# A two-layer decoder trunk on one core: gate products behind the value projection, kept weight blocks from the MLP's twelfth block on, and four of the inverse's eight late stores on GpSimd's queue

## The chip, the cores and the metric

The kernel runs on one core of a Trainium2 chip. The metric is the device time of one execution in microseconds, the median of several runs.

## The reference, cut to what matters

A trunk of two layers on 512 tokens of 1024 features, in float32. Layer 0 is sparse attention, layer 1 an RWKV-7 mixer; each is followed by an MLP with a squared ReLU of 4096 hidden features. The change touches the first MLP and the RWKV mixer:

```python
def sqrelu_mlp(h, w_up, w_down):
    u = jax.nn.relu(h @ w_up)
    return (u * u) @ w_down
...
r, k, v = jnp.einsum('cbld,cde->cble', xs[:3], w_rkv)
...
g = jax.nn.sigmoid(xg @ g1) @ g2
...
def step(state, inp):                      # over the 512 tokens, 16 heads of 64
    r_t, w_t, k_t, v_t, kk_t, b_t = inp
    sa = jnp.einsum('bhvk,bhk->bhv', state, -kk_t)
    state = (state * w_t[:, :, None, :] + sa[..., None] * b_t[:, :, None, :]
             + v_t[..., None] * k_t[:, :, None, :])
    y = jnp.einsum('bhvk,bhk->bhv', state, r_t)
    return state, y
...
out = (y + bonus).reshape(B, L, D).astype(h.dtype) * g
return out @ w_o
```

## The kernel before, in words

**Weights.** All weights come as blocks of 128 x 1024 float32 in one stream, in the order of the table `c.order`. `wdma` (L92) loads one or two blocks on SyncE's (SP's) queue; `wload` splits a block into a high part by a copy on ScalarE (L109) and a low part by a subtraction on VectorE (L117); `gemm` (L135 to L137) makes 24 matmuls of a block. `wget` keeps two blocks ahead, always in stream order, so the splits stand in that order on ScalarE and VectorE too. 24 blocks of the RWKV mixer (the list `PRE`) are split early: the table puts them in pairs into the first MLP's part of the stream, `pos` marks them, and `keep` (L79) stores both halves of each into DRAM (tiles `scr`) by GpSimd's (POOL's) queue. Later SP loads them back (L85), 1 MB each.

**The first MLP** (`mlp`). For each half of the hidden features, 16 blocks of the first product, m = 0 to 15, each followed by the activations of `act`: VectorE L287, ScalarE L289 and L290, VectorE L291. Then eight products down, of two blocks each. `keep` is called behind every fourth block m of the first product and behind every second of the second one, in the first half only. In the stream, position 26 is the MLP's first block.

**The RWKV mixer.** Tokens go in eight chunks of 64. For each chunk and head, a triangular 64 x 64 matrix has to be inverted, by blocks of 32. `back` (L1015) masks the matrices into the tiles `Mt`; `invert` puts them into DRAM (`dn`, L1029, eight stores for the first eight heads, eight for the others) and loads them back with one matrix per partition (`tn`, L1034, one load for each half f of the chunks). 60 VectorE operations (L1041, L1043) invert all of them. Copies (L1049) and stores and loads through DRAM (`dm`, `dt`) bring the results back as `Mt` and `T11`. Meanwhile PE makes the value projection (192 matmuls, L1229 to L1231, eight PSUM banks) with inputs prepared on VectorE and ScalarE (L753, L120, L117, L751), and `opl` and `opt` make the operands of a chunk: products on PE (L1201, L1202), masks on VectorE (L1196), transposes (L1213) with copies (L1214, and `cp`: L1133 on VectorE, L1135 on ScalarE). Each of these steps has its place in the queues from priorities and the scheduler, up to the line `c.tc.manual_schedule`.

**From there on all five engines follow the order in which the code is written.** First come the copies of the values (`vcopy`, L1241), the gate products (`g2`, L1259 to L1262, 4 matmuls for each of 8 parts), and the preparation of the first chunk: `step_z` (L1290, copied into `bd` by ScalarE L1292), `merge1` (L1143), `merge2` (L1155, copied into `Mt` by ScalarE L1135). Then the loop over the chunks n: `step_z`, `step_u` (L1298, copied by ScalarE L1302), `merge1` of the next, `step_s` and `step_n` (L1309, L1316: the next state), `step_r` (L1327) and `step_y` (L1340, copied by ScalarE L1345: the output), `opl` of the next, `merge2`, `opt`.

PSUM has two pools: four banks "g" and two double banks "d". A tile waits until the one that had its bank has been read.

Of the kernel before, what the change touches and what calls it, by code (L numbers as in the profile page):

```python
# [7 lines left out]
F32 = mybir.dt.float32  # L8
F32R = mybir.dt.float32r
AF = mybir.ActivationFunctionType  # L10
# [266 lines left out]
def mlp(c, x, mi, done, mid, keep=0):  # L277
    nc = c.nc
    c.ph = 'm'
    a = mi.a  # L280
    rstd = None
    wait = []

    @c.site("mact")
    def act(p, hi, lo):
        r = c.t("r")
        nc.vector.scalar_tensor_tensor(r, p, 0.0, rstd, op0=OP.max, op1=OP.mult)  # L287
        q = c.t("q")
        nc.scalar.activation(hi, r, AF.Square)  # L289
        nc.scalar.activation(q, r, AF.Square)  # L290
        nc.vector.tensor_sub(lo, q, hi.bitcast(F32))  # L291

    for half in range(2):
        s = Act(c, "s", 16)
        for m in range(16):
            p = c.bank("g")
            c.gemm(p, c.wget(), a)
            if m % 4 == 3:
                c.keep(keep)
            wait.append((p, *s(m)))  # L300
            if rstd is None:
                if m == 0:
                    mi.n.stat()
                    continue
                rstd = mi.n.spread()
            while wait:
                act(*wait.pop(0))
        for m in range(KC - HM if half else KC):
            p = c.bank("g")
            c.gemm(p, c.wget(), s, last=False)  # L310
            c.gemm(p, c.wget(), lambda k: s(k + 8), first=False)
            if m % 2 and not half:
                c.keep(keep)
            xm = x[m // 4][:, m % 4, :]
            nc.vector.tensor_add(xm, p, xm)  # L315
            if half:
                for h in range(2):
                    done(m, xm[:, HB[h]], h)
    w = [c.wget(1) for _ in range(2 * HM)]
    for h in range(2):  # L320
        for i in range(HM):
            m = KC - HM + i
            p = c.bank("g")[:, :256]
            for j in range(2):
                c.gemm(p, w[2 * i + j], lambda k: [v[:, HB[h]] for v in s(k + 8 * j)], j == 0, j == 1)
                if h:
                    next(mid, None)
            xm = x[m // 4][:, m % 4, HB[h]]
            nc.vector.tensor_add(xm, p, xm)
            done(m, xm, h)  # L330
    for _ in mid:
        pass
# [453 lines left out]
def rwkv(c, x, ks, gi):  # L786
# [232 lines left out]
    def invert():  # L1019
        dn, dm = (c.dram.tile([2, 2, 2, 32, 32, 32], F32, name=v) for v in ("dn", "dm"))  # L1020
        dt = c.dram.tile([2, 2, 32, 32, 32], F32, name="dt")
        mt = [t.rearrange("p q n t -> p (q n) t") for t in Mt]
        for q in range(2):
            qs = slice(16 * q, 16 * q + 16)
            for f in range(2):
                for e in range(2):
                    for b in range(2):
                        r = slice(e * 64 + b * 32, e * 64 + b * 32 + 32)
                        nc.sync.dma_start(dn[f, e, b, qs].rearrange("h i j -> i h j"),  # L1029
                                          mt[f][r, qs, b * 32:b * 32 + 32])  # L1030
            yield HOLD
        tn = c.b8("tn", F32, (128, 2, 32, 32))
        for f in range(2):
            nc.sync.dma_start(tn[:, f].rearrange("p i j -> p (i j)"), dn[f].rearrange("e b h i j -> (e b h) (i j)"))  # L1034
        yield HOLD
        pr = c.t("pr")
        for k in range(30, 0, -1):
            nr = 31 - k
            sh = [128, 2, k, nr]
            pv = pr[:, :2 * k * nr].rearrange("p (f a b) -> p f a b", f=2, a=k)  # L1040
            nc.vector.tensor_mul(pv, tn[:, :, 0:k, k:k + 1].to_broadcast(sh),  # L1041
                                 tn[:, :, k:k + 1, k + 1:].to_broadcast(sh))
            nc.vector.tensor_add(tn[:, :, 0:k, k + 1:], tn[:, :, 0:k, k + 1:], pv)  # L1043
            yield 4 * (k * nr * 1.04 + 65)
        for f in range(2):
            nc.vector.memset(tn[:, f].rearrange("p i j -> p (i j)")[:, 0:1024:33], 1.0)
            tt = [c.t("tt").rearrange("p (i j) -> p i j", j=32) for _ in range(2)]
            for g in range(2):
                nc.vector.tensor_copy(tt[g], tn[:, f].rearrange("p i j -> p j i")[:, 16 * g:16 * g + 16])  # L1049
            if f == 0:  # L1050
                stage.append(0)
                yield HOLD
            nc.sync.dma_start(dm[f].rearrange("e b h i j -> (e b h) (i j)"), tn[:, f].rearrange("p i j -> p (i j)"))
            for e in range(2):
                for g in range(2):
                    nc.sync.dma_start(dt[f, e, :, 16 * g:16 * g + 16], tt[g][e * 64:e * 64 + 32])
            yield HOLD
            T11[f] = [c.t("T11").rearrange("p (h j) -> p h j", j=32) for _ in range(2)]
            for e in range(2):
                for g in range(2):  # L1060
                    nc.sync.dma_start(T11[f][g][e * 64:e * 64 + 32],
                                      dt[f, e, g * 16:(g + 1) * 16].rearrange("h i j -> i h j"))
                for b in range(2):
                    r = slice(e * 64 + b * 32, e * 64 + b * 32 + 32)
                    nc.sync.dma_start(mt[f][r, :, b * 32:b * 32 + 32], dm[f, e, b].rearrange("h i j -> i h j"))
            yield HOLD
# [360 lines left out]
    def opn(n, j):  # L1427
        if j == 0:
            BL[n] = c.b8("BL", F32, (128, 2, 8, 128))
        opl(n, j)  # L1430

    with c.tc.manual_schedule(engines=set(MAN)):
        while not stage:
            run(1)
        until(0)
        for i in VL[:3]:
            vcopy(i)
        vmean(0)
        vload(0)
        opn(1, 0)  # L1440
        for i in VL[3:]:
            vcopy(i)
        del ps
        opn(1, 1)
        (ah, al_), (bh, bl) = ((a.rearrange("p a b -> p (a b)") for a in c.wget(0)) for _ in range(2))
        nc.scalar.activation(bh[64:96], bl[64:96].bitcast(F32), AF.Copy)
        g2(0)
        g2(1)
        step_z(0)
        g2(2)  # L1450
        g2(3)
        opt(1, (0, 0))
        vload(1)
        g2(4)
        g2(5)
        sa[0] = merge1(0)
        g2(6)
        merge2(0, sa[0])
        g2(7)
        for n in range(NCH - 1):  # L1460
            more = True
            if n:
                step_z(n)
            if n % 2 and more:
                vmean((n + 1) // 2)
            if n == 1:
                lnw = g3(c.t("lnw"))
                nc.sync.dma_start(lnw, c.aps["lnw"])
            if n and more:
                acopy(n + 1)  # L1470
                opn(n + 1, 0)
                vload(n + 1)
            if n == 6:
                turn(3)
            for k in GB.get(n, ()):
                gB(k)
            step_u(n)
            if n == 0:
                until(1)
            if more and n != 3:  # L1480
                sa[n + 1] = merge1(n + 1)
            for k in GB.get(n, ()):
                gC(k)
            if more:
                pn = step_s(n)
                step_n(n, pn)
            py = step_r(n)
            if more:
                sbd(n)
            step_y(n, py)  # L1490
            for k in GB.get(n, ()):
                gD(k)
            if n == 6:
                w0 = out(0)
                pull(w0, 1)
            if n and more:
                opn(n + 1, 1)
            if n == 6:
                pull(w0, 2)
            if n == 3:  # L1500
                sa[4] = merge1(4)
            if more:
                merge2(n + 1, sa[n + 1])
            if n and n < NCH - 2:
                opt(n + 1, (0, 0) if n < 3 else TE)
            for k in TU.get(n, ()):
                turn(k)
            for k in GA.get(n, ()):
                gA(k)
            if n == PF1:  # L1510
                c.prefetch(2)
# [130 lines left out]
def build(tc, aps, out):  # L1642
    with ExitStack() as ctx:
# [4 lines left out]
        for i in range(26, BASE):  # L1648
            od.append(i)
            pos.append(0)  # L1650
            if i % 4 == 1:
                pos += [1] * len(pre[:2])
                od += pre[:2]
                del pre[:2]
# [43 lines left out]
```

## Time and profile before

| | |
|---|---|
| median of 3 runs | 1360.39 us (1356.75 to 1364.64) |
| profiled execution | 1363.17 us, its span 1361.0 us |
| mean granted TensorE clock | 0.982 |
| PE busy | 1294.1 us, 95% |
| DVE, ACT, POOL busy | 778.1, 593.5, 191.8 us |
| first MLP | about 265 to 620 us |
| inverse and value projection | about 774 to 827 us |
| chunk loop | about 845 to 960 us |

The table is read with the span: the rows further down come from the one profiled execution and are times from the start of its span. "Busy" counts matmuls for PE; the weight loads run beside them. The granted clock is a share of 2.4 GHz.

### The profile page before, as it was taken

How to read it: one execution, taken by the hardware profiler on the slowest of the kernel's cores; microseconds unless marked ns; L12 is line 12 of the kernel's file. 1: busy time of each engine (PE TensorE's matmuls, PEld its weight loads, DVE VectorE, ACT ScalarE, POOL GpSimd, SP SyncE). 2: the span in 40 equal slices, each digit the busy share in tenths (PEclk: the TensorE clock that was granted, in tenths of full speed). 3: DMA queues.
4: the chain of work that ended last, by engine and by line, in shares of the span. 5: the costliest groups of instructions: out<-in, count | busy, mean ns of one | idle time of the engine just before them, and what ended most of it. 6: DMA issues, size and time to landing. Idle time of an engine off the chain costs nothing.

```text
span 1361.0 us, 20178 instructions
## 1 busy us (share of the span) xinstructions
PE 1294.1 (95%) x8197; PEld 1060.0 (78%) x8197; DVE 778.1 (57%) x1345; ACT 593.5 (44%) x1016; POOL 191.8 (14%) x220
## 2 busy tenths in 40 slices
PE   7989899999999999999999998877999999999997
PEld 6756666878888888899667776766988888888887
DVE  5689983646542556428889785564754532245423
ACT  5545693434432345316875315755343421234421
POOL 0375750001101010000000001253200000000000
PEclk9989999989999999999999998988999999999998
DMA  7101004345677666413241375127131223322401
GB/s 290 63 23 40 1 14 173 116 155 216 228 270 245 246 220 254 144 63 124 78 155 40 94 286 108 28 80 279 53 103 62 93 95 108 108 92 93 155 1 62
DMA packets 73404, 172.09 MB, mean 126 GB/s; under 512 B 33760, under 2 KB 36448, under 8 KB 69472
## 3 DMA queue, kind: packets, MB, share of 16 engines
q1 hardware_dynamic: 64160, 143.41, 30.8%
q0 software_dynamic: 6912, 25.17, 5.1%
q10 hardware_dynamic: 2240, 2.24, 0.5%
q8 instruction: 64, 1.05, 0.3%
q14 instruction: 28, 0.23, 0.0%
HBM read 136.72 MB, written 31.98 MB: 124 GB/s over the span
## 4 chain that ended last, share of the span: by engine, by line
PE 79%; DVE 12%; ACT 4%; issue 2%; DMA 2%; POOL 1%; SPq 1%; DVEq 0%; ACTq 0%; POOLq 0%
PE g L137 20%; PE g L135 20%; PE g L136 20%; PE g L648 2%; DVE rot L431 1%; DVE tn L1043 1%; DVE pr L1041 1%; PE d L633 1%; DVE acc L517 1%; DVE L L607 1%; DVE m L515 1%; PE g L1298 1%; PE g L1013 1%; ACT bd L1292 1%; PE d L406 1%
## 5 line engine op out<-in xcount | busy, mean ns | idle before, releaser
L117 DVE TENSOR_TENSOR w<-wraw,w 128x1024 fp32r<-128x1024 f32 x185 | 224.2, 1239 | 125.9 <-ACT w L109 125.9
L109 ACT ACTIVATE w<-wraw 128x1024 fp32r<-128x1024 f32 x190 | 193.0, 1048 | 141.4 <-DMA wraw<-in_wblk 119.1
L135 PE MATMUL g<-sh,w 128*128 128x512 f32 (+1 forms) x608 | 216.5, 356 | 0.0
L136 PE MATMUL g<-sl,w 128*128 128x512 f32 (+1 forms) x608 | 216.1, 355 | 0.0
L137 PE MATMUL g<-sh,w 128*128 128x512 f32 (+1 forms) x608 | 216.1, 355 | 0.0
L135 PE MATMUL g<-ah,w 128*128 128x512 f32 x512 | 201.0, 393 | 2.9 <-ACT w L109 2.9
L137 PE MATMUL g<-ah,w 128*128 128x512 f32 x512 | 200.3, 391 | 0.0
L136 PE MATMUL g<-al,w 128*128 128x512 f32 x512 | 200.3, 391 | 0.0
L289 ACT ACTIVATE sh<-r 128x512 fp32r<-128x512 f32 x64 | 40.4, 631 | 205.3 <-DVE r L287 205.3
L136 PEld LDWEIGHTS g<-sl,w 128*128 128x128 f32 x608 | 114.9, 189 | 16.4
L135 PEld LDWEIGHTS g<-sh,w 128*128 128x128 f32 x608 | 114.9, 189 | 16.2
L137 PEld LDWEIGHTS g<-sh,w 128*128 128x128 f32 x608 | 114.9, 189 | 16.2
L135 PEld LDWEIGHTS g<-ah,w 128*128 128x128 f32 x512 | 96.8, 189 | 23.1 <-ACT w L109 3.3
L137 PEld LDWEIGHTS g<-ah,w 128*128 128x128 f32 x512 | 96.8, 189 | 21.0 <-DVE w L117 0.8
L136 PEld LDWEIGHTS g<-al,w 128*128 128x128 f32 x512 | 96.9, 189 | 20.1
L287 DVE SCALAR_TENSOR_TENSOR r<-g,rstd 128x512 f32<-128x512 f32 x64 | 44.1, 691 | 82.1 <-PE g L137 70.5
L291 DVE TENSOR_TENSOR sl<-q,sh 128x512 fp32r<-128x512 f32 x64 | 44.4, 694 | 75.4 <-ACT q L290 75.4
L195 ACT ACTIVATE sq<-x 128x256 f32<-128x256 f32 (+1 forms) x56 | 26.7, 499 | 98.1 <-DVE x L315 52.2
L79 POOL DMA_DIRECT2D scr<-w x48 | 25.6, 536 | 295.9 <-ACT w L109 285.8
L315 DVE TENSOR_TENSOR x<-g,x 128x512 f32<-128x512 f32 x26 | 17.9, 690 | 80.6 <-PE g L137 80.6
L617 ACT ACTIVATE L<-L,st 128x256 f32<-128x256 f32 (+3 forms) x64 | 35.1, 552 | 15.1 <-DVE st L615 15.1
L290 ACT ACTIVATE q<-r 128x512 f32<-128x512 f32 x64 | 39.4, 615 | 0.0
(317 smaller groups left out, 2425.7 us busy)
## 6 DMA issues: line engine op xcount, KB each, us to landing
wraw<-in_wblk SPq DMA_DIRECT2D x94, 1024.0 KB, 5.0
scr<-w POOLq DMA_DIRECT2D x48, 512.0 KB, 4.1
w<-scr SPq DMA_DIRECT2D x24, 1024.0 KB, 6.7
wraw<-in_wblk SPq DMA_DIRECT2D x5, 512.0 KB, 3.9
x<-in_xT SPq DMA_DIRECT2D x8, 256.0 KB, 5.3
x<-in_xT SPq DMA_DIRECT2D x2, 1024.0 KB, 6.6
xs<-x SPq DMA_DIRECT2D x2, 1024.0 KB, 5.0
abd<-AR SPq DMA_DIRECT2D x64, 32.0 KB, 2.6
```

What stands on the lines that cost most here:

```text
L109: s.wsp = s.nc.scalar.activation(hi, r, AF.Copy)
L117: s.nc.vector.tensor_sub(out, a, b)
L135: s.nc.tensor.matmul(p, whi[:, kc, :], ahi, start=first and kc == 0, stop=False)
L136: s.nc.tensor.matmul(p, whi[:, kc, :], alo, start=False, stop=False)
L137: s.nc.tensor.matmul(p, wlo[:, kc, :], ahi, start=False, stop=last and kc == KC - 1)
L195: nc.scalar.activation(sq, xk, AF.Square)
L287: nc.vector.scalar_tensor_tensor(r, p, 0.0, rstd, op0=OP.max, op1=OP.mult)
L289: nc.scalar.activation(hi, r, AF.Square)
L290: nc.scalar.activation(q, r, AF.Square)
L291: nc.vector.tensor_sub(lo, q, hi.bitcast(F32))
L617: nc.scalar.activation(L[g][:, :n], L[g][:, :n], AF.Exp, bias=nmx[:, g:g + 1], scale=0.125, accum_out=sm[:, g:g + 1])
L648: nc.tensor.matmul(po[HF[e]], v[sc // 2][:, j:j + 64], st8[tb, pr, e][:, sc], start=sc == 0, stop=sc == tb)
```

## The change

The diff has four parts. In `mlp`, `keep` is called in the second half too; in the table, the pairs of kept blocks start at position 37 instead of 29, and end at 81 instead of 73. In `invert`, the four stores of the last eight whose e is 1 go to GpSimd's queue. Behind the value projection, the weights of the gate products are fetched first, all eight `vcopy` and four `g2` come before the operands of chunk 1, and the rest follows in another order. In the chunk loop, `step_r` is called before `step_u`.

```diff
@@ mlp
-            if m % 2 and not half:
+            if m % 2:
                 c.keep(keep)
@@ invert
-                        nc.sync.dma_start(dn[f, e, b, qs].rearrange("h i j -> i h j"),
+                        (nc.gpsimd if q and e else nc.sync).dma_start(dn[f, e, b, qs].rearrange("h i j -> i h j"),
                                           mt[f][r, qs, b * 32:b * 32 + 32])
@@ rwkv
     with c.tc.manual_schedule(engines=set(MAN)):
+        (ah, al_), (bh, bl) = ((a.rearrange("p a b -> p (a b)") for a in c.wget(0)) for _ in range(2))
+        nc.scalar.activation(bh[64:96], bl[64:96].bitcast(F32), AF.Copy)
         while not stage:
             run(1)
         until(0)
-        for i in VL[:3]:
+        for i in VL:
             vcopy(i)
+        del ps
         vmean(0)
         vload(0)
+        for m in range(4):
+            g2(m)
         opn(1, 0)
-        for i in VL[3:]:
-            vcopy(i)
-        del ps
-        opn(1, 1)
-        (ah, al_), (bh, bl) = ((a.rearrange("p a b -> p (a b)") for a in c.wget(0)) for _ in range(2))
-        nc.scalar.activation(bh[64:96], bl[64:96].bitcast(F32), AF.Copy)
-        g2(0)
-        g2(1)
-        step_z(0)
-        g2(2)
-        g2(3)
-        opt(1, (0, 0))
-        vload(1)
         g2(4)
         g2(5)
+        step_z(0)
+        opn(1, 1)
+        vload(1)
         sa[0] = merge1(0)
+        opt(1, (0, 0))
         g2(6)
         merge2(0, sa[0])
         g2(7)
@@ rwkv, loop over n
             if n == 6:
                 turn(3)
+            py = step_r(n)
             for k in GB.get(n, ()):
                 gB(k)
             step_u(n)
...
                 step_n(n, pn)
-            py = step_r(n)
             if more:
                 sbd(n)
             step_y(n, py)
@@ build
-            if i % 4 == 1:
+            if i % 4 == 1 and i > 34:
                 pos += [1] * len(pre[:2])
```

Three places show how this moves instructions. The first is ScalarE's queue at the start of the first MLP, before. The rows L289 and L290 are a block's activations, L109 the splits; the first two L109 are kept blocks, the third is the split of block m = 4.

```order
L289 ACTIVATE sh_2304<-r_2435 128x512
L290 ACTIVATE q_2437<-r_2435 128x512
L109 ACTIVATE w_2408<-wraw_2406 128x1024
L109 ACTIVATE w_2442<-wraw_2406 128x1024
L289 ACTIVATE sh_2304<-r_2481 128x512
L290 ACTIVATE q_2483<-r_2481 128x512
L109 ACTIVATE w_2471<-wraw_2469 128x1024
```

The same place now; the first L109 is the split of m = 4, the next two are m = 5 and 6.

```order
L289 ACTIVATE sh_2304<-r_2393 128x512
L290 ACTIVATE q_2395<-r_2393 128x512
L109 ACTIVATE w_2406<-wraw_2357 128x1024
L289 ACTIVATE sh_2304<-r_2399 128x512
L290 ACTIVATE q_2401<-r_2399 128x512
L289 ACTIVATE sh_2304<-r_2433 128x512
L290 ACTIVATE q_2435<-r_2433 128x512
L109 ACTIVATE w_2442<-wraw_2440 128x1024
L109 ACTIVATE w_2476<-wraw_2440 128x1024
```

The split of m = 4 stood behind the activations of m = 3 (r_2481), and now stands behind those of m = 0 (r_2393).

The second place is SP's queue at the inverse's start, as a difference: dn are the stores of the matrices, tn the two loads, w the blocks read back, abd a chunk's operands.

```order
-L1029 DMA dn<-Mt 32x16x32 x6
+L1029 DMA dn<-Mt 32x16x32 x4
 L1034 DMA tn<-dn 128x1024
-L1029 DMA dn<-Mt 32x16x32 x2
 L1168 DMA abd<-AR 64x2x64
+L1034 DMA tn<-dn 128x1024
 L85 DMA w<-scr_2288 128x2048
-L1034 DMA tn<-dn 128x1024
 L1168 DMA abd<-AR 64x2x64 x7
```

Four stores have left the queue, and the second tn stands ahead of the 1 MB load. On POOL's queue the four now stand between two memsets:

```order
 L943 MEMSET seg 128x8
+L1029 DMA dn<-Mt 32x16x32 x4
 L1250 MEMSET bd 128x2048
```

Nothing else on POOL's queue changes its place there.

The third place is VectorE's queue at the same time, now. L1133 is the copy that `opt` of chunk 0 makes out of its PSUM bank, L1041 and L1043 are the inverse, L753 and L117 the preparation of the projection's inputs.

```order
L1196 TENSOR_TENSOR BL<-d,kon 128x4x64 x4
L1041 TENSOR_TENSOR pr<-tn 128x60
L1043 TENSOR_TENSOR tn<-tn,pr 128x2x30
L1041 TENSOR_TENSOR pr<-tn 128x116
L753 SCALAR_TENSOR_TENSOR xm<-h,vec,xm 128x511
L1043 TENSOR_TENSOR tn<-tn,pr 128x2x29x2
L1041 TENSOR_TENSOR pr<-tn 128x168
L1043 TENSOR_TENSOR tn<-tn,pr 128x2x28x3
L117 TENSOR_TENSOR xl<-xm,xh 128x512
L1041 TENSOR_TENSOR pr<-tn 128x216
L753 SCALAR_TENSOR_TENSOR xm<-h,vec,xm 128x511
L1043 TENSOR_TENSOR tn<-tn,pr 128x2x27x4
L1133 COPY BL<-d 64x8x64
```

Before, L1133 stood directly behind the masks L1196 and ahead of the first L1041. In the chunk loop and behind the projection the queues follow the diff.

## Rows read from the trace of the kernel before

**Rows 1.** The page, part 1: busy time of each engine, its share of the span, instructions.

```profile
PE 1294.1 (95%) x8197; PEld 1060.0 (78%) x8197; DVE 778.1 (57%) x1345; ACT 593.5 (44%) x1016; POOL 191.8 (14%) x220
```

**Rows 2.** What TensorE waited for between 280 and 640 us (the first MLP): engine and line, the releaser, us in total, number of waits, the longest.

```profile
PE g L135 <- ACT w L109: 2.9, 1, 2.9
```

**Rows 3.** TensorE's timeline around that wait, fourth and fifth block of the first MLP: start, duration (both us), engine, line, operation, names and shapes.

```profile
289.22 0.39 PE L136 MATMUL g<-al,w 128*128 128x512 f32 x1
...
295.02 0.63 PE L136 MATMUL g<-al,w 128*128 128x512 f32 x1
295.45 0.63 PE L137 MATMUL g<-ah,w 128*128 128x512 f32 x1
...
299.22 0.39 PE L137 MATMUL g<-ah,w 128*128 128x512 f32 x1
...
300.14 0.40 PE L135 MATMUL g<-ah,w 128*128 128x512 f32 x1
```

**Rows 4.** Stretches of the span: from:to and length, busy us (and instructions) of PE, of its weight loads, DVE, ACT and POOL, then the granted TensorE clock (share of full speed), the DMA engines' busy share and GB/s.

```profile
270.00:290.00 20.00, 19.83 (x100) 16.48 (x98) 7.38 (x14) 7.96 (x12) 1.84 (x4) 1.00 0.23 83
290.00:310.00 20.00, 17.21 (x62) 13.54 (x63) 8.75 (x10) 8.22 (x12) 0.48 (x1) 0.83 0.53 187
370.00:400.00 30.00, 30.00 (x134) 24.85 (x133) 13.13 (x13) 8.45 (x9) 3.75 (x8) 1.00 0.85 303
824.00:846.00 22.00, 16.81 (x216) 12.95 (x216) 8.74 (x23) 12.74 (x23) 4.17 (x4) 0.84 0.69 143
```

**Rows 5.** TensorE's timeline from the value projection (L1229 to L1231) to the first chunk step (L1298).

```profile
789.32 0.50 PE L1229 MATMUL d<-w,xh 128*128 128x512 f32 x1
...
823.90 0.39 PE L1231 MATMUL g<-w,xl 128*128 128x512 f32 x1
...
830.49 0.44 PE L1201 MATMUL d<-AR,KB 64*64 64x128 f32 x1 [5.17 <-DVE BL L1196]
...
832.99 0.63 PE L1260 MATMUL g<-sg,w 128*128 128x512 f32 x1
833.42 0.63 PE L1261 MATMUL g<-sg,w 128*128 128x512 f32 x1
...
845.28 1.09 PE L1298 MATMUL g<-bd,Mt 128*64 128x128 f32 x16
```

**Rows 6.** What TensorE waited for between 846 and 965 us (the chunk loop), the first line of the answer: us in total, number, the longest.

```profile
PE g L1298 <- ACT bd L1292: 12.6, 7, 2.9
```

**Rows 7.** ScalarE's timeline at the start of the first MLP; in square brackets the idle time ahead and what ended it.

```profile
286.22 1.99 ACT L109 ACTIVATE w<-wraw 128x1024 fp32r<-128x1024 f32 x2
290.60 0.63 ACT L289 ACTIVATE sh<-r 128x512 fp32r<-128x512 f32 x1 [2.39 <-DVE r L287]
...
291.65 2.94 ACT L109 ACTIVATE w<-wraw 128x1024 fp32r<-128x1024 f32 x3
```

**Rows 8.** SyncE's queue at the inverse's start, its DMA-issuing instructions: start, time to issue, line, tiles, number.

```profile
774.62 4.67 SPq L1029 DMA_DIRECT2D dn<-Mt  x6
779.94 0.34 SPq L1034 DMA_DIRECT2D tn<-dn  x1
...
784.66 0.34 SPq L1034 DMA_DIRECT2D tn<-dn  x1
```

**Rows 9.** The chain that ended last, from 770 to 850 us, three of its pieces: start, duration, what.

```profile
776.06 3.69 DMA dn<-Mt
780.81 3.78 DMA dn<-Mt
...
832.57 2.09 DMA T<-dt
```

**Rows 10.** VectorE's timeline around the inverse's start.

```profile
783.57 1.40 DVE L1196 TENSOR_TENSOR BL<-d,kon 128x256 f32<-128x256 f32 x4
787.95 0.68 DVE L1133 COPY BL<-d 64x512 f32<-64x512 f32 x1 [2.98 <-ACT BL L1214]
...
789.85 0.27 DVE L1041 TENSOR_TENSOR pr<-tn 128x60 f32<-128x60 f32 x1 [1.21 <-DMA abd<-AR]
...
793.25 0.38 DVE L1043 TENSOR_TENSOR tn<-tn,pr 128x216 f32<-128x216 f32 x1
```

**Rows 11.** The page, part 5 (the kept blocks' stores: number, busy us and mean ns to issue one) and part 6 (transfers: number, KB each, median us from issue to landing); the last line is the landing time over all transfers of the tiles scr.

```profile
L79 POOL DMA_DIRECT2D scr<-w x48 | 25.6, 536 | 295.9 <-ACT w L109 285.8
...
wraw<-in_wblk SPq DMA_DIRECT2D x94, 1024.0 KB, 5.0
scr<-w POOLq DMA_DIRECT2D x48, 512.0 KB, 4.1
...
DMA to landing us min/median/max: 2.9/5.1/14.1
```

**Rows 12.** DMA issues between 774 and 786 us, one line: number, KB each, median us to landing.

```profile
tn<-dn SPq DMA_DIRECT2D x2, 512.0 KB, 4.4
```

**Rows 13.** TensorE's timeline in the chunk step n = 4: step_r and step_y.

```profile
896.77 1.04 PE L1327 MATMUL g<-bd,AR 128*64 128x128 f32 x16
897.65 1.15 PE L1340 MATMUL g<-sv,BL 128*64 128x64 f32 x32
```

**Rows 14.** ScalarE's timeline in the same step: the copies of y and of Mt.

```profile
899.17 0.60 ACT L1345 ACTIVATE y<-g 128x512 f32<-128x512 f32 x1
900.50 0.76 ACT L1135 ACTIVATE Mt<-g 32x256 f32<-32x256 f32 x2 [0.73 <-PE g L1155]
```

## The prediction

> **What bounds the kernel now.** I read the page first: TensorE (PE) is busy 95% of the span [rows 1], so time is to be had only where PE stands or runs at its lower clock. The waits of PE stretch by stretch then show three such places. In the first MLP, PE waits once between 280 and 640 us, 2.9 us for a weight split on ScalarE [rows 2]. The timeline around that wait shows its second price: the reader should see starts 0.43 us apart for some 6 us behind it, and 0.23 again from 299.22 on [rows 3]; the granted clock of those 20 us is 0.83, of the 20 before 1.00 [rows 4], so 2.4 GHz gave way to 1.2 for a while after PE had stood. Behind the value projection PE stands 5.17 us and again goes on at starts 0.43 us apart [rows 5]. In the chunk loop step_u waits for ScalarE's bd seven times, 12.6 us [rows 6].
>
> **Part 1, the kept blocks start eight positions later.** The stall has one cause. On ScalarE the split of stream block m4 (the first of three L109 at 291.65) is queued behind the activations of m3 (290.60), which wait for m3's own matmuls; the two L109 at 286.22 that belong to kept blocks pushed it there [rows 7]. In the changed order m4's split stands behind the activations of m0, and the first kept pair comes at m11, where the split of m12 stands behind the activations of m10, one block (24 x 0.23 = 5.5 us) earlier than it is needed. The price comes from the starts: from 289.22 to 300.14 PE makes 20 steps [rows 3], which at 0.23 us take 4.6 and took 10.9, so 6.3 us are lost, 2.9 of them standing and the rest at the lower clock. **-6.3 us.** The bounds are -6.3 and, if the later kept pairs stall once themselves, 0. What is moved: 48 transfers on POOL's queue and their splits on ScalarE and VectorE, now running some 8 x 5.5 = 44 us longer at the end. Their cover is PE: from 370 to 400 us the same traffic ran beside it with DMA at 0.85, 303 GB/s, and PE full at clock 1.00 [rows 4], and the later stretch has less of it. SP is moved too: the store of xs now stands ahead of two more raw loads, which by my reading of the order still leave about two blocks, 11 us, ahead of their use, against 5.0 us to landing [rows 11].
>
> **Part 2, four of the inverse's stores by POOL.** Before, SP issues six dn stores from 774.62 (4.67 us), stands until the first half has landed, issues tn's first half at 779.94, then the last two dn [rows 9], and tn's second half only at 784.66 [rows 8]; the chain shows the two landings, 3.69 and 3.78 us, one behind the other [rows 9]. The inverse's first VectorE operation starts at 789.85 [rows 10]; call this moment T. With four stores on each queue the two halves land together. Best case: SP done by 777, POOL's four at the 0.53 us of its nearest row [rows 11] also by 777, landing 3.7 [rows 9], tn 4.4 [rows 12]: T = 785.4. Bad case: POOL's issue grows with the pieces, 512 of 128 bytes against 128 rows, 2.1 us each: 774.9 + 8.6 + 3.7 + 4.4 = 791.6. No row prices such a store on POOL; I take T = 787, nearer the row that exists. On this point the Trainium skill speaks against the change: "DMA: Bandwidth & Descriptors" (section "Latency and other measured facts") puts the first byte of a DMA issued by GpSimd at about 1 us and of one issued by SP at about 0.6. By it T would be 0.4 us later; no run here shows the two queues with one size: POOL's 512 KB land in 4.1 us and SP's 1 MB in 5.0 [rows 11].
>
> T alone does not set the end; **a wait is added**. The copy L1133 (before at 787.95, ahead of the inverse [rows 10]) and ScalarE's L1135 behind it now stand behind eight inverse operations and three preparations on VectorE. Before, that many with one preparation fewer took 789.85 to 793.63 [rows 10]; with it 4.4, then 0.68 and 0.59 for the two copies: the PSUM bank is free at T + 5.8. Value products queue for it on PE, and behind them all the rest of the projection. Before, they went on at 789.32 and ended at 824.13, 34.8 us later [rows 5]. So the projection ends at T + 40.6, at T = 787 3.5 us later than before. Its stall of 3.2 us at 789.6 lies beside one of 2.9 us that cost the clock [rows 2, 4]; the clock took 6.3 - 2.9 = 3.4 us there, and I put half of that, +1.7, on it. Inverse work itself is covered: 36 us on VectorE under 34.8 on PE.
>
> **Part 3, gate products behind the projection.** What PE waits for at 830.49 is VectorE, which does the inverse's tail, its copies (L1049) and the mean (L1275) before the masks (L1196). In the new order eight vcopies and four g2 stand between, whose inputs are there long before. From the projection's end to step_u is 845.28 - 824.13 = 21.15 us [rows 5]. Of that 5.2 is standing (22.00 - 16.81 [rows 4]), and some 2.0 is the lower clock: six g2 matmuls at 0.43 instead of 0.23, and the masks' products. The rest, 14.0, is work that stays. I add 0.3 for the copy of Mt, which has less between now: 14.3. The first T11 landed at 834.66 [rows 9], 44.8 us behind T, now some 0.7 later for L1133; merge1 needs it at T + 50: covered by 4 us. So step_u comes at T + 54.9 = 841.9 against 845.28. **Parts 2 and 3 together: -3.4 + 1.7 = -1.7 us**, bounds -5.0 (T = 785.4) and +4.6 (T = 791.6 with the full 3.4).
>
> **Part 4, step_r ahead of step_u.** step_r takes 0.88 us (896.77 to 897.65 [rows 13]) and moves from behind step_n into the wait before step_u. Seven waits sum to 12.6 [rows 6]; the longest, 2.9, is the last step's, where nothing moves, so six waits with 9.7 us can take it: at most 6 x 0.88 = -5.3. The other end is 0: ScalarE is what step_u waits for, and behind step_n its row is bd, y (899.17), then the copy of Mt (900.50) [rows 14]. With merge2 0.88 earlier the copy can begin only when y ends, 899.77 instead of 900.50: 0.7 of 0.88 is passed on there, less where VectorE comes last. I take 0.5 for each: **-3.0 us**.
>
> Sum: -6.3 - 1.7 - 3.0 = -11.0 us. The profiled execution took 1363.17 for a span of 1361.0, 2.8 above the median 1360.39; the difference is taken from the median: **1349**.
>
> **The rivals.**
> *The loop gives nothing back.* ScalarE sets the period of a chunk step and step_r only fills a wait that returns elsewhere. For: all seven waits end on ScalarE. Against: merge2's result, which ScalarE copies, does come earlier. -8.0 us: 1352.
> *POOL is held up by VectorE.* VectorE works almost without a break until its masks end at 784.97 [rows 10], and if POOL's stores come out only then: 785 + 2.1 + 3.7 + 4.4 gives T = 795.2, step_u at 850.1, +4.8, and 3.4 of clock. Sum -6.3 + 8.2 - 3.0 = -1.1: 1359. "SBUF — State Buffer" of the Trainium skill (section "SBUF: two separate sides") has this as a trap: a DMA issued by GpSimd cannot have its descriptors written while VectorE runs a copy in its two-port mode. Against it here: the work in that stretch is two-input arithmetic and one copy out of PSUM, not SBUF copies, and in MLP1 POOL's stores landed in 4.1 us [rows 11].
> *The MLP's stall only moves.* If m12's split comes late as m4's did, part 1 is worth 0: -4.7, 1356. Against: kept pairs in the middle of the old stream never stalled PE: there is one wait in 360 us [rows 2].
> *Slower: the four stores on POOL decide.* They issue at 2.1 us each and land as late as the slowest transfer of the kept blocks, 14.1 us [rows 11]: T = 774.9 + 8.6 + 14.1 + 5.2 = 802.8, step_u at 857.7, +12.4, and 3.4 of clock behind a stall of 19 us. With nothing from the loop: -6.3 + 15.8 = +9.5: 1370. It decides from T = 793.3 on, where that sum is zero, and is beyond +6.8 from T = 800.1. For: no row shows POOL with such small pieces. Against: each of them moves 64 KB, an eighth of a kept block.
>
> **How the numbers follow.** A measurement of this kernel can tell about 0.5%, 6.8 us, from no change. Forecast 0.55, the loop rival 0.15: both faster, 0.70. POOL held up 0.13 and the moved stall 0.10: within 0.5%, 0.23. Slower 0.07. The range starts at -6.3 - 5.0 - 5.3 = -16.6 with another 2 us, as three runs spread by 8: 1342. It ends at 1358, near the second rival, and leaves out the slower case and the tail of that rival.
>
> **What would show it.** In the changed profile: no PE wait for L109 between 280 and 640 and clock 1.00 in 290 to 310; four dn on POOL at 775, both tn issued by 783, first L1041 near 787; a PE wait for the bank of L1229 at about 790; no 5 us idle behind the projection and step_u 55 us behind T; the waits of step_u for bd down from 12.6 to about 7. Wrong would be a wait at m12, POOL stores landing after 790, or waits of step_u that shrink while others of PE in the loop grow as much.

## The result, and the profile after

The changed kernel takes **1349.99 us**, the median of 4 runs (1346.70 to 1350.72); the kernel before, run beside it, 1361.54 (1356.75 to 1364.64, 4 runs). The ratio is 0.991, 95% interval 0.9886 to 0.9934. The forecast was 1349 in 1342 to 1358. The profiled execution has a span of 1348.9 us, 12.1 less than before.

To see where the 12.1 us come from, I cut both traces at four matmuls that both have: the first of MLP 1, the first of the mixer (L909), the first of step_u(0) and of step_u(7) (L1298). The numbers are starts, and differences between starts; the last row runs to the end of the span.

| stretch, us | before | after | difference | forecast |
|---|---|---|---|---|
| up to the first MLP (untouched) | 265.14 | 266.30 | +1.2 | 0 |
| first MLP to L909 (part 1) | 414.30 | 409.24 | **-5.1** | -6.3 |
| L909 to step_u(0) (parts 2, 3) | 165.84 | 163.76 | **-2.1** | -1.7 |
| step_u(0) to step_u(7) (part 4) | 92.39 | 86.71 | **-5.7** | -3.0 |
| the rest (untouched) | 423.33 | 422.94 | -0.4 | 0 |

The first row is no effect of the change: over all profiles taken it lies between 262.3 and 266.8. So whole times of single runs can't carry a microsecond here. The second row can: two profiles of the changed kernel give 409.24 both times. The third row can't: there the same two profiles give 163.76 and 161.84, and the experiments show why.

**Part 1.** The waits of PE from 280 to 640 us, and the stretches that answer to [rows 4], in the changed kernel:

```profile
PE g L137 <- DVE w L117: 1.0, 1, 1.0
```

```profile
290.00:310.00 20.00, 20.00 (x90) 16.57 (x89) 8.72 (x11) 7.28 (x11) 0.00 (x0) 1.00 0.16 52
310.00:370.00 60.00, 58.99 (x261) 48.51 (x260) 32.47 (x36) 25.97 (x35) 6.04 (x11) 1.00 0.58 203
790.00:794.00 4.00, 4.00 (x12) 3.08 (x12) 3.97 (x8) 1.48 (x3) 0.00 (x0) 0.59 1.01 420
825.40:839.30 13.90, 13.43 (x202) 10.33 (x201) 4.24 (x11) 9.89 (x20) 3.72 (x4) 1.00 0.47 99
839.30:926.01 86.71, 75.33 (x1809) 62.55 (x1809) 52.04 (x113) 58.55 (x123) 36.78 (x33) 0.98 0.42 116
```

The wait of [rows 2] is gone, and 290 to 310 us are full at clock 1.00 instead of 17.21 at 0.83. In its place stands one of 1.0 us, between 310 and 370, for the low part of a split. VectorE's timeline at that point shows why, with the PE matmul that waits:

```profile
334.55 0.69 DVE L287 SCALAR_TENSOR_TENSOR r<-g,rstd 128x512 f32<-128x512 f32 x1 [1.88 <-PE g L137]
335.16 2.35 DVE L117 TENSOR_TENSOR w<-wraw,w 128x1024 fp32r<-128x1024 f32 x2
```

```profile
336.43 0.50 PE L137 MATMUL g<-ah,w 128*128 128x512 f32 x1 [1.01 <-DVE w L117]
```

The subtraction for m12 is the first of the two L117, behind the activation L287 of m11, which waits for m11's own matmuls: the old stall in small, on VectorE instead of ScalarE. No lower clock followed it.

**Part 2.** SP's queue and POOL's at the inverse's start, and the DMA issues of 768 to 784 us (number, KB, median us to landing), to be held against [rows 8, 9, 12]:

```profile
770.73 3.62 SPq L1029 DMA_DIRECT2D dn<-Mt  x4
776.23 0.34 SPq L1034 DMA_DIRECT2D tn<-dn  x1
...
777.56 0.45 SPq L1034 DMA_DIRECT2D tn<-dn  x1
778.10 0.38 SPq L85 DMA_DIRECT2D w<-scr  x1
```

```profile
771.00 2.62 POOL L1029 DMA_DIRECT2D dn<-Mt  x4 [70.32 <-DVE Mt L1015]
```

```profile
w<-scr SPq DMA_DIRECT2D x1, 1024.0 KB, 8.8
dn<-Mt SPq DMA_DIRECT2D x4, 64.0 KB, 4.1
dn<-Mt POOLq DMA_DIRECT2D x4, 64.0 KB, 4.3
```

POOL issues a store in 0.66 us and it lands like SP's. Both tn go out 1.3 us apart (before 4.7). But the 1 MB of weights behind them now takes 8.8 us to land; in the kernel before the same line reads:

```profile
w<-scr SPq DMA_DIRECT2D x1, 1024.0 KB, 5.9
```

PE in the changed kernel, from those weights to step_u(0), and VectorE's first inverse operation and L1133 (answering to [rows 5, 10]):

```profile
787.06 0.76 PE L1229 MATMUL g<-w,xh 128*128 128x512 f32 x1 [3.07 <-DMA w<-scr]
787.62 0.63 PE L1230 MATMUL g<-w,xh 128*128 128x512 f32 x1
788.05 0.63 PE L1231 MATMUL g<-w,xl 128*128 128x512 f32 x1
...
825.21 0.39 PE L1231 MATMUL g<-w,xl 128*128 128x512 f32 x1
```

```profile
782.46 0.26 DVE L1041 TENSOR_TENSOR pr<-tn 128x60 f32<-128x60 f32 x1 [2.16 <-DMA tn<-dn]
...
786.81 0.68 DVE L1133 COPY BL<-d 64x512 f32<-64x512 f32 x1
```

To compare, I count from the end of the last mask of Mt (774.93 before, 771.03 after). T moves from 14.9 to 11.4 us, the projection's end from 49.2 to 54.4: PE stands 3.07 us for the weights and then goes on at starts 0.43 us apart, clock 0.59 from 790 to 794. An earlier wait, for the masks of chunk 0, got shorter; before it was 2.2 us:

```profile
PE d L1213 <- DVE BL L1196: 1.4, 1, 1.4
```

**Part 3.** From the projection's end (825.44) to step_u(0) (839.30) it is 13.9 us instead of 21.15, PE busy 13.43 of 13.90 at clock 1.00.

**Part 4.** The loop's two largest waits of PE, answering to [rows 6]:

```profile
PE g L1298 <- ACT bd L1292: 5.5, 4, 2.9
PE g L1290 <- DVE abd L1196: 4.0, 2, 2.2
```

### The profile page after: what moved, and what is told of

Same layout as the page of the kernel before. It is cut to its first block, busy times and chain, and to the rows that moved or that the text cites. A ratio compares the mean times of both kernels' runs of the same rounds, so it can differ in the third digit from the quotient of the medians.

```text
span 1348.9 us, 20186 instructions
## 1 busy us (share of the span) xinstructions
PE 1291.6 (96%) x8197; PEld 1057.4 (78%) x8197; DVE 777.8 (58%) x1345; ACT 592.6 (44%) x1016; POOL 194.6 (14%) x224
## 4 chain that ended last, share of the span: by engine, by line
PE 83%; DVE 10%; ACT 4%; issue 2%; POOL 1%; DMA 1%; SPq 0%; DVEq 0%; ACTq 0%; POOLq 0%
PE g L137 20%; PE g L136 20%; PE g L135 20%; PE g L648 2%; DVE rot L431 1%; PE d L633 1%; DVE acc L517 1%; DVE L L607 1%; DVE m L515 1%; DVE w L117 1%; DMA w<-scr 1%; PE g L1298 1%; PE g L1013 1%; PE d L404 1%; PE d L406 1%
## 5 line engine op out<-in xcount | busy, mean ns | idle before, releaser
L117 DVE TENSOR_TENSOR w<-wraw,w 128x1024 fp32r<-128x1024 f32 x185 | 224.3, 1239 | 126.0 <-ACT w L109 125.9
L109 ACT ACTIVATE w<-wraw 128x1024 fp32r<-128x1024 f32 x190 | 192.7, 1048 | 143.4 <-DMA wraw<-in_wblk 120.6
L289 ACT ACTIVATE sh<-r 128x512 fp32r<-128x512 f32 x64 | 40.4, 631 | 201.9 <-DVE r L287 201.9
L287 DVE SCALAR_TENSOR_TENSOR r<-g,rstd 128x512 f32<-128x512 f32 x64 | 44.1, 691 | 85.4 <-PE g L137 73.6
L617 ACT ACTIVATE L<-L,st 128x256 f32<-128x256 f32 (+3 forms) x64 | 35.1, 552 | 16.6 <-DVE st L615 16.6
L290 ACT ACTIVATE q<-r 128x512 f32<-128x512 f32 x64 | 39.4, 616 | 0.0
```

Source lines behind the costliest of these rows:

```text
L109: s.wsp = s.nc.scalar.activation(hi, r, AF.Copy)
L117: s.nc.vector.tensor_sub(out, a, b)
L617: nc.scalar.activation(L[g][:, :n], L[g][:, :n], AF.Exp, bias=nmx[:, g:g + 1], scale=0.125, accum_out=sm[:, g:g + 1])
```

## The experiments

All are counted as above: T, the projection's end (V) and step_u(0) from the last Mt mask, and the stretch from L909, in two parts. One table for all, from one profile each:

| kernel | MLP 1 | T | V | V to step_u(0) | step_u(0) | L909 to mask | L909 to step_u(0) | loop | time (runs) |
|---|---|---|---|---|---|---|---|---|---|
| before | 414.30 | 14.9 | 49.2 | 21.2 | 70.3 | 95.5 | 165.8 | 92.4 | 1361.54 (4) |
| changed | 409.24 | 11.4 | 54.4 | 13.9 | 68.3 | 95.5 | 163.8 | 86.7 | 1349.99 (4) |
| after_again | 409.24 | 11.4 | 52.5 | 13.9 | 66.3 | 95.5 | 161.8 | 86.6 | 1349.26 (6) |
| u_stores_sp | 409.26 | 15.6 | 49.2 | 16.7 | 65.8 | 95.5 | 161.4 | 86.3 | 1346.87 (6) |
| u_old_order | 409.25 | 11.7 | 52.4 | 15.6 | 68.0 | 95.5 | 163.5 | 86.5 | 1349.26 (4) |
| u_r_late | 409.25 | 14.3 | 56.3 | 13.9 | 70.2 | 93.9 | 164.1 | 92.3 | 1351.40 (6) |
| u_keep_early | 413.55 | 10.7 | 50.8 | 13.9 | 64.6 | 95.5 | 160.2 | 86.4 | 1351.60 (4) |
| w_first | 409.25 | 11.8 | 46.4 | 18.1 | 64.5 | 95.5 | 160.0 | 86.9 | 1345.83 (5) |
| stores_sp_w_first | 409.26 | 13.3 | 47.1 | 18.4 | 65.5 | 93.9 | 159.4 | 86.3 | 1344.05 (6) |
| stores_pool_8 | 409.25 | 15.8 | 49.6 | 16.6 | 66.1 | 95.5 | 161.6 | 86.4 | 1348.83 (1) |
| first_kept_single | 407.91 | 10.9 | 50.9 | 13.9 | 64.8 | 93.9 | 158.7 | 86.4 | 1343.81 (1) |
| only_stores_pool | 414.34 | 11.3 | 52.7 | 15.6 | 68.3 | 95.5 | 163.8 | 92.3 | 1360.58 (1) |
| only_g2_order | 413.57 | 15.5 | 49.4 | 16.5 | 65.9 | 95.5 | 161.4 | 91.0 | 1353.78 (1) |
| sp_w_first_single | 407.91 | 13.7 | 47.5 | 18.4 | 65.9 | 93.9 | 159.8 | 87.1 | 1343.27 (4) |

Two things have to be known to read it. PE's order from L909 to the masks is the same in all of these profiles, yet this stretch takes 95.5 us in ten and 93.9 in four. The difference is the granted clock at one place, some 8 to 13 us ahead of the last mask, here in u_stores_sp and stores_sp_w_first:

```profile
756.00:761.00 5.00, 5.00 (x32) 4.06 (x32) 3.89 (x8) 0.00 (x0) 0.00 (x0) 0.66 0.01 3
```

```profile
754.00:759.00 5.00, 5.00 (x42) 4.26 (x42) 2.48 (x6) 1.17 (x2) 0.00 (x0) 1.00 0.60 213
```

The edits do not sort the profiles this way: first_kept_single has 93.9 and after_again, with the same queues there, 95.5. So the column to compare for parts 2 and 3 is step_u(0) from the mask. And five of the profiles, changed, after_again, u_r_late, u_keep_early and first_kept_single, have the same instructions in the same order on all five queues from the masks to step_u(0). Their step_u(0) comes at 64.6 to 70.2 us (mean 66.8), as the wait for the weights takes 1.5 to 4.2 us and the lower clock follows it in three of the five. A difference of 2 us between two single profiles shows nothing here.

**u_stores_sp: the change without part 2.**

```diff
-                        (nc.gpsimd if q and e else nc.sync).dma_start(dn[f, e, b, qs]...
+                        nc.sync.dma_start(dn[f, e, b, qs]...
```

> The change without part 2: all eight late dn stores on SP's queue again, the rest as changed. Theory: the stores on POOL and the gate products behind the projection remove the same 5 us of standing, and the stores pay for it in the projection, where the 1 MB of weights and the copy L1133 now come behind the inverse's start. Counted from the end of the last Mt mask, the projection should end at about 49 us (changed kernel 54.4) and step_u(0) start at about 65 us (68.3), with one new wait of up to 2 us of merge1 for T11; the time falls by about 3 us against the changed kernel, to about 1347. Rival: the earlier start of the inverse is what lets the chunk loop start early; without it step_u starts 3 to 4 us later than in the changed kernel, about 1353.

Measured: V 49.2, step_u(0) 65.8, a wait for T11 of 1.3 us; 1346.87, ratio to before 0.9916 (0.9894 to 0.9938). The waits of PE from 755 to 850 us:

```profile
PE d L1213 <- DVE BL L1196: 2.2, 1, 2.2
PE g L1143 <- DMA T<-dt: 1.3, 1, 1.3
```

The weights are not among them, so the price in the projection is shown, and the rival falls: step_u(0) is not later than in the five profiles of the changed order (64.6 to 70.2). That the time falls by 3 us is not shown: 65.8 lies within those, and the whole times (1346.16 to 1352.55, after_again 1344.83 to 1349.99) do not separate the two. Given part 3, no gain of part 2 is shown.

**u_old_order: the change without part 3** (the block behind the projection as in the kernel before).

> The change without part 3: behind the projection the instructions stand in the old order. Theory: with the inverse started early VectorE is done with its tail before the projection ends, so the masks come in time in the old order too: no standing of 5 us, projection end to step_u(0) about 14 us (changed kernel 13.9), time within 1 us of the changed kernel. Rival: the order itself is what removes the standing; 21 us from the projection's end to step_u, 7 us slower than the changed kernel, about 1357.

Measured: V to step_u(0) 15.6 us, not 21. PE's waits there:

```profile
PE g L1229 <- DMA w<-scr: 2.4, 1, 2.4
PE d L1201 <- DVE BL L1196: 1.7, 1, 1.7
```

The standing of [rows 5] has shrunk from 5.2 to 1.7 without the new order: the rival falls, though the 14 us expected were missed too. The time, 1349.26, is the changed kernel's.

**only_stores_pool and only_g2_order: the kernel before with part 2, or part 3, alone.**

> The kernel before with part 2 alone: four late dn stores on POOL. Theory: the earlier start of the inverse removes most of the 5.2 us of standing behind the projection also in the old order, but the projection pays 2 to 5 us for it; from the mixer's first matmul to step_u(0) 163 to 165 us (before 165.8, changed kernel 163.8 and 161.8), from the projection's end to step_u about 15.6. Rival: without part 3 the standing stays, 21 us from the projection's end to step_u and 168 to 170 in all, slower than before.

> The kernel before with part 3 alone: gate products ahead of the masks. Theory: it removes the standing by itself, from the projection's end to step_u about 16.7 us with a wait of about 1.3 us for T11, the projection unchanged (49.2 us behind the last Mt mask); from the mixer's first matmul to step_u(0) 161.4 us against 165.8. Rival: it needs the earlier inverse, and PE stands for the masks or T11 for 4 us or more: 164 us.

Measured, in one run each: part 2 alone brings step_u(0) 2.0 us nearer to the mask and pays 3.5 in the projection for it; part 3 alone brings it 4.5 nearer and leaves V where it was, 0.2 apart. Together they bring 0.1 to 5.7 in the five profiles of the changed order, 3.5 in the mean. Of the standing of 5.2 us at L1201, part 2 alone leaves 1.7 and part 3 alone none. So both remove the same standing; part 3 does so without the wait for the weights, at the price of 1.6 us of waiting for T11.

**u_r_late: the change without part 4.**

```diff
-            py = step_r(n)
             for k in GB.get(n, ()):
                 gB(k)
...
                 step_n(n, pn)
+            py = step_r(n)
```

> The change without part 4: step_r behind step_n again. Theory: the loop from step_u(0) to step_u(7) takes 92.4 us as in the kernel before (changed kernel 86.7), so +5.7 us, about 1355.7, and the waits of step_u for bd come back to about 12 us. Rival: part of the gain in the loop belongs to the new start ahead of it and to a clock that fell less often by chance; +3 us, 1353, with the loop at about 89.5 us.

Measured: the loop is back at 92.3 us, and so are the waits of step_u:

```profile
PE g L1298 <- ACT bd L1292: 11.7, 6, 2.9
```

The whole time, 1351.40 (1347.02 to 1357.37), is less than the 1355.7 expected; the interval of its ratio to before, 0.9914 to 0.9959, overlaps that of the changed kernel, 0.9886 to 0.9934. By the loop the rival's 89.5 us falls. But its point on the clock holds for a part: only_g2_order, also with the old loop, takes 91.0 us.

**u_keep_early: the change without part 1** (positions from 29 on, `keep` in the first half only).

> The change without part 1: the pairs of kept blocks start at position 29 again. Theory: the wait of 2.9 us for L109 and the stretch at the lower clock come back, the wait of 1.0 us at the twelfth block goes; +5.1 us, about 1355. Rival: the later stretch of kept blocks costs elsewhere (the end of the MLP, the read-back), so that the whole gain of part 1 is smaller; +3 us, 1353.

Measured: MLP 1 takes 413.55 us, 4.3 more, with these waits of PE from 280 to 640:

```profile
PE g L135 <- ACT w L109: 2.9, 1, 2.9
PE g L137 <- DVE w L117: 0.5, 1, 0.5
```

That is less than the 5.1 between the kernel before and the changed one, though the wait is the same 2.9 us: the lower clock behind it was shorter here, 0.91 over these 20 us instead of 0.83 [rows 4].

```profile
290.00:310.00 20.00, 16.56 (x65) 12.85 (x64) 9.53 (x12) 7.44 (x11) 1.61 (x3) 0.91 0.60 214
```

So part 1 is worth 4.3 to 5.1 us. The whole time rose by less than expected (1351.60); in this profile the projection waited 1.5 us for its weights, half as long as in the changed kernel's first one.

**w_first: the changed kernel with the weight load ahead of the stores.**

```diff
     run(1)
+    c.prefetch(3)
     run(1)
     acopy(0)
-    c.prefetch(3)
```

> The changed kernel with c.prefetch(3) called between the two run(1) ahead of the chunk operands, so that SP issues the 1 MB of weights that the projection needs at its third block ahead of the last dn stores. Theory: in the changed kernel the wait of PE for these weights (3.1 us, and the lower clock behind it) is the price of part 2, because the load runs beside tn and abd; issued ahead of dn it is there in time. The projection ends about 50 to 51 us behind the last Mt mask (changed kernel 54.4, late stores on SP 49.2), step_u(0) at about 64 to 65 (68.3), about 4 us faster than the changed kernel, 1346. Rival: the wait moves to the bank that L1133 frees behind the inverse's first operations, or dn and tn land later by as much; projection end at 53 or later, no gain over 1 us.

Measured: SP issues the load at 751.43, 15 us ahead of dn; it lands in 4.8 us. PE no longer waits for it, V is the earliest of all (46.4, in the five profiles of the changed order 50.8 to 56.4), and step_u(0) comes at 64.5, at the early end of the changed order's 64.6 to 70.2. The time, 1345.83 (ratio 0.9888, 0.9872 to 0.9904), stands against 1349.26 for the changed kernel measured beside it (0.9903, 0.9887 to 0.9919): less, but the intervals overlap. What PE waits for next, from 755 to 850 us, is T11:

```profile
PE g L1143 <- DMA T<-dt: 2.0, 1, 2.0
PE g L1290 <- POOL sv L1282: 0.4, 1, 0.4
```

**after_again: the changed kernel once more.**

> The changed kernel once more, on the chip of the runs beside it. Theory: T at about 11.4 us behind the last Mt mask, PE waits 2 to 4 us for the third weights of the projection, step_u(0) at about 68 us; time 1350, slower than the version with the late stores on SP (1347) by 2 to 3 us. Rival: the wait for the weights in the first profile was a single event; without it step_u(0) comes at 65 us and the time is 1347.

Measured: T the same 11.4, the wait 2.3 us instead of 3.1, step_u(0) at 66.3 instead of 68.3. The wait is no single event: all seven profiles with four stores on POOL and the load behind tn show PE standing there, 1.5 to 4.2 us, as the load takes 7.3 to 9.9 us to land (the 4.2, in u_r_late, is put down to ScalarE, which prepares the next input behind VectorE's inverse; but the load landed just 0.14 us before PE went on):

```profile
w<-scr SPq DMA_DIRECT2D x1, 1024.0 KB, 9.9
```

**stores_sp_w_first: both edits.**

> The same earlier weight load, with all dn stores on SP. Theory: there the weights were never waited for (projection end 49.2 us behind the last Mt mask), so the load moved ahead gains nothing of its own: step_u(0) at 65 to 66 us, within 1 us of the version with the stores on SP. With L1133 now behind two inverse operations, a T of 15 us would even hold PE for about 2 us: projection end 49 to 52. Rival: the load ahead frees the DMA engines for tn, T comes 2 us earlier, and this is the fastest version.

Measured: 1344.05, ratio 0.9871 (0.9851 to 0.989). The projection ends earlier than expected, at 47.1: with the weights there, the order puts four more products ahead of the transposes, and the 2.2 us of waiting at L1213 that u_stores_sp shows are filled. But step_u(0) comes at 65.5, only 0.4 us earlier than in u_stores_sp, as expected: behind the projection it now takes 18.4 us instead of 16.7, part of them at the lower clock. The stretch from L909 is shorter by 2.0 us, of which 1.6 is the clock ahead of the masks. The rival was right in that T comes 2.3 us earlier and that this is the lowest time so far. The whole times differ by more than step_u(0) does (1346.87 to 1344.05); that this is the edit's doing is not shown.

**stores_pool_8: all eight late stores on POOL.**

> All eight late dn stores on POOL's queue. This prices one store of 512 pieces of 128 bytes there: my row for the forecast was 0.53 us each, the changed profile shows 2.62 us for four, 0.66 each. Theory: eight take about 5.3 us and land some 4.3 us behind their issue, so T comes 13 to 14 us behind the last Mt mask, about 2 us later than with four on each queue. Rival: descriptors of the later stores queue up behind one another, 2 us each, and T comes at 20 us or later.

Measured, POOL's issue and the landing (DMA issues of 766 to 790 us):

```profile
770.84 5.18 POOL L1029 DMA_DIRECT2D dn<-Mt  x8 [70.29 <-DVE Mt L1015]
```

```profile
dn<-Mt POOLq DMA_DIRECT2D x8, 64.0 KB, 2.9
```

They take 0.65 us each to issue, and land faster than the 4.3 us expected. T at 15.8 is later than the 13 to 14 expected, since tn's second half is issued behind the weights again; the rival's 20 falls.

**first_kept_single: one kept block at position 37, three at 57.**

```diff
-                pos += [1] * len(pre[:2])
-                od += pre[:2]
-                del pre[:2]
+                g = {37: 1, 57: 3}.get(i, 2)
+                pos += [1] * len(pre[:g])
+                od += pre[:g]
+                del pre[:g]
...
-        mlp(..., k.first(), 2)
+        mlp(..., k.first(), 3)
```

> The changed kernel with one kept block instead of two at position 37 and three at position 57. Theory: the wait of 1.0 us at the MLP's thirteenth block is the low part of its split, queued on VectorE behind the activations of the block just ahead, because the pair of kept blocks moved it there; with one kept block it stands earlier. The wait goes, the first MLP from its first matmul to the mixer's first one (409.25 us in the changed kernel, 414.30 before) takes 408.2; no new wait at the three blocks, where the products are twice as long. Rival: the wait returns at the later place, 409.3 or more.

Measured: no wait of PE between 280 and 640 us, MLP 1 takes 407.91, 1.3 less than in the changed kernel and 6.4 less than before.

**sp_w_first_single: what the runs point to.**

> The version that the runs point to: the change without part 2, the third weights of the projection loaded ahead of the late stores, and one kept block at position 37. Theory: 1.0 us less than the version without the last edit (1344.1), so about 1343, faster than both kernels. Rival: the last edit gives nothing, 1344 to 1345.

Measured: 1343.27 (1340.66 to 1344.27), ratio 0.9863 (0.9838 to 0.9888), against 0.9903 (0.9887 to 0.9919) for the changed kernel, measured at another time. It beats the kernel before clearly. It lies about 6 us below the changed one; the intervals of the two ratios just touch, and no run of one lies among those of the other. From stores_sp_w_first the whole times do not separate it.

## Why the forecast held, step by step

The time came out at the forecast, but two of its three terms did not. Their errors, +1.2 and -2.7 us, cancel in part, and the third term came out near its forecast by another path than the one forecast. So the closeness of the sum is luck in part.

*Part 1, forecast -6.3, measured -5.1.* The cause of the old stall was right, and its price too: without any new wait the stretch shrinks by 6.4 (first_kept_single, again in sp_w_first_single). What failed is the step "the split of m12 stands behind the activations of m10". That is so on ScalarE, where I had read the order; the low part is made on VectorE, and there it stands behind m11's. A wait at m12 had been named as a sign of being wrong, and it came: the rival "the stall only moves" was true for 1.0 us of it, without the fall of the clock.

*Part 2, forecast T = 787.* On the changed kernel's scale (3.9 us earlier at the masks) that is 783.1; T came at 782.46. The nearest row for POOL's issue, 0.53, was close to the 0.66 measured, and the bad case of 2.1 and the two rivals on POOL fall: POOL issued its first store at 771.00, while VectorE was at work until 780.3. Small slips in the sums (785.4 holds 0.3 that the other cases for T lack, and the terms of 5.8 add up to 5.7) change nothing.

The Trainium skill ("DMA: Bandwidth & Descriptors", section "Latency and other measured facts") gives the first byte of a DMA at about 1 us when GpSimd issues it and about 0.6 us when SP does; by that, as an estimate, the start by POOL would be 0.4 us later. The trace shows landings, not first bytes, and they differ by 0.2 us (medians of 4.3 and 4.1). The trap in the Trainium skill's page "SBUF — State Buffer" (section "SBUF: two separate sides"), a DMA of GpSimd held up while VectorE runs a copy in its two-port mode, was not put to the test: beside the stores, 4.3 us to landing, VectorE worked on two-input arithmetic and one copy out of PSUM.

*The added wait.* I put a stall of 3.2 us at the bank that L1133 frees. The bank came as worked out (L1133's copy done at 787.49, ScalarE's L1135 at 788.12, 5.7 us behind T), but PE already stood for the weights until 787.06 and ran at the lower clock behind that; no wait for the bank shows. In five other profiles it does show, at 0.6 to 1.0 us, as here in first_kept_single:

```profile
PE d L1229 <- ACT BL L1135: 0.6, 1, 0.6
```

The weight load has no term in the prediction: I never asked when it lands, though the order showed tn ahead of it. Which of the transfers beside it takes its 2.9 us more was not separated. Behind this other stall the clock's price, taken at 1.7, was 2.9: the 14 steps from 787.06 to 793.17 take 6.1 us instead of 3.2. V came 5.2 us later: 3.1 of standing and 2.9 of clock, less the 0.8 by which the wait at L1213 got shorter. This is also why the -2.1 for parts 2 and 3 is near its forecast by luck: in the five profiles of the same order the gain at step_u(0) is 0.1 to 5.7.

*Part 3, forecast 14.3 us from V to step_u(0), measured 13.9.* Right, and steady: 13.9 in all five. But I gave the whole standing to part 3 and never asked what either part would do alone. The experiments show one standing of 5.2 us with two remedies.

*Part 4, forecast -3.0 within 0 to -5.3, measured -5.7.* The mechanism held, and the rival "the loop gives nothing back" falls. But the term is mis-sized, because the clock was put at nothing. From step_u to step_u the loop's seven intervals shrink by 0.0, 0.9, 0.9, 0.7, 1.4, 1.9 and 0.0 us. The first has nothing to give: step_r(0) is empty in the code. The next three ran at clock 1.00 in both kernels. The two large ones exceed the 0.88 us of step_r. In the kernel before, the loop runs at 0.96:

```profile
845.28:937.67 92.39, 75.81 (x1809) 63.12 (x1808) 51.62 (x113) 58.98 (x123) 36.83 (x33) 0.96 0.33 95
```

and in the changed one at 0.98. In step n = 5 PE stood 2.5 us before step_u, and step_s behind it took 1.98 us:

```profile
908.66 1.09 PE L1298 MATMUL g<-bd,Mt 128*64 128x128 f32 x16 [2.52 <-ACT bd L1292]
...
910.42 1.98 PE L1309 MATMUL g<-bd,ident 128*64 128x512 f32 x4
```

In the changed kernel the same two rows, with no wait ahead:

```profile
898.90 1.16 PE L1298 MATMUL g<-bd,Mt 128*64 128x128 f32 x16
...
900.61 1.08 PE L1309 MATMUL g<-bd,ident 128*64 128x512 f32 x4
```

How much of the two is clock can be read where the old loop kept its clock there: the fifth interval in only_g2_order, the sixth in u_r_late.

```profile
884.42:899.99 15.57, 11.72 (x272) 9.59 (x272) 11.95 (x24) 8.68 (x19) 8.01 (x7) 1.00 0.52 159
```

```profile
904.76:918.00 13.24, 11.92 (x280) 10.18 (x280) 8.52 (x22) 9.08 (x20) 9.58 (x10) 1.00 0.11 17
```

The changed kernel takes 15.57 and 12.77 for them, so step_r itself gives 0.0 and 0.5 there. Its share of the 5.7 is then 2.9 us, next to the forecast of 3.0, and the clock's is 2.8. As this sets intervals of different kernels side by side, and the first of the two ran at 0.90 in the changed kernel, the split is an estimate. In the steps n = 4 and 6 the gain goes into waits for VectorE's masks: L1290 waits 4.0 us where it was 2.6.

## What to carry to other kernels

A split that is made on two engines has two places in two queues; follow both before you call a stall gone. Two edits that end the same wait do not add up: alone they brought 2.0 and 4.5 us, together 3.5 in the mean. So ask of each what it would do alone, and what it pays: here the queue change was paid for by a load that had just been in time. Work moved into a wait can be worth more than its own length, where the wait cost the clock as well. And before you read 2 us off two profiles, look how far profiles of the same queues differ in that stretch: here it was 5.6 us.

## What the runs showed of the hardware

A store of 512 pieces of 128 bytes costs 0.65 us to issue on POOL, little more than one of 128 rows of 4 KB (0.54 [rows 11]): the number of pieces hardly counted.

The same load of 1 MB lands in 4.7 to 4.9 us when it is issued some 14 to 15 us ahead of the stores (three profiles), in 5.9 to 7.7 between the two halves of tn (four), and in 7.3 to 9.9 behind both (seven).

After 3.1 us without work PE ran at starts of 0.43 us instead of 0.23, clock 0.59 from 790 to 794 us, as it had after 2.9 us in the first MLP. At the same place, behind waits of 1.5 and 1.6 us (u_keep_early, first_kept_single), the clock stayed at 1.00. The same wait of 2.9 us in the first MLP left 20 us at 0.83 in one profile and at 0.91 in another, so one wait does not have one price.
